# Splitting the first load of a sum of rectified rows: one row of each partition ahead of the other fifteen

## The chip, the cores and the metric

The kernel runs on one core of one Trainium2 chip. The metric is the device time of one execution in microseconds (us). Before the change it is 161.06 us, the median of three runs (161.24, 160.89 and 161.06).

## What is computed

The input `x` has the shape 32 x 512 x 1024 in float32, 67.1 MB. Every row of 1024 numbers is clamped at zero and summed:

```python
relu_x = np.maximum(x, 0)
return np.sum(relu_x, axis=-1).astype(np.float32)
```

There are 16,384 rows and as many sums, so 64 KB are written for 67.1 MB that are read.

## The kernel before

**Tiling.** The 16,384 rows are laid over 128 partitions, 128 rows to each. A block is 16 rows of every partition: 128 x 16 x 1024 float32, 8 MB, and 64 KB in one piece of memory for each partition. There are eight blocks. The first seven (`NB = 7`) are each loaded by one DMA into one of three buffers `io0` to `io2`, in turn (`NBUF = 3`). The eighth is cut into ever smaller loads: 8 rows, 4 rows, and the last four rows in four loads of 1164, 642, 120 and 122 KB, the last two into small tensors of their own (`piece0`, `piece1`).

**Two ways to sum a row.** The blocks that `TWO` lists are done in two steps: `clamp` (L117) has ScalarE (ACT in the profile) apply relu to a whole stretch of rows in place, and `total` (L125) has VectorE (DVE) reduce the stretch to one sum per row, after it has waited for the clamp. Single rows are done in one instruction, either on ACT (`act_row`, L132) or on DVE (`dve_row`, L140), with a short second instruction that reads the accumulator. `TWO = [[16], [16], [16], [8, 8], [8, 8], [7, 7], []]` gives the stretches of each block; block 0 is thus one clamp of 16 rows and one reduce of 16 rows. The seventh block and the eighth are done row by row on both engines.

**Order.** All DMAs are issued by SyncE (SP; its queue is SPq in the profile) by `load` (L99) and `store` (L110), in program order. A load into a buffer that was used before waits until DVE has counted up to the value in `freed`, which is the number of DVE instructions done when the older block of that buffer is finished. So the first three loads wait for nothing, and load 3 waits for block 0. Each load has a semaphore of its own; `act` and `dve` count the instructions of the two engines. Three stores write the sums: of block 0, of all that follows but two, and of the last two.

**The opening.** `open_without_barrier` (L238 and after) takes the first `EARLY = 1` load of SP's program out of the body and puts it ahead of SP's other instructions in the opening block. The second load and those after it stay in the body.

Of the kernel before, what the change touches and what calls it, by code (L numbers as in the profile page):

```python
# [9 lines left out]
ROWS = 16  # L10
NBUF = 3


TWO = [[16], [16], [16], [8, 8], [8, 8], [7, 7], []]
ACT = [0, 0, 0, 0, 0, 2, 9]
DVE = [0, 0, 0, 0, 0, 0, 7]

# [2 lines left out]
TAIL = [8, 4]  # L20
START_PIECE, END_PIECE = 280, 260
PIECES = [240, 244]

EARLY = 1


def kernel(tc: tile.TileContext, x: bass.AP, out: bass.AP):
    nc = tc.nc
    sems = Semaphores(tc)

    tc.close()
    tc.compile()
    nc.cur_bb = nc.bb_map[tc.start_bb_name]
    body = nc.cur_bb.bb.instructions
    ends = list(body)
    body.clear()
    n_stores = relu_sum(nc, sems, x, out)
    body.extend(ends)


    nc.cur_bb = nc.bb_map[tc.start_bb_name + "_end"]
    nc.cur_bb.bb.instructions.clear()
    nums = sorted(s.num for s in (*sems.loads, sems.act, sems.dve))
    cleared = range(nums[0], nums[-1] + 1)
    assert len(cleared) == len(nums)
    nc.sync.sem_clear(cleared)
    nc.sync.wait_ge(sems.stored, 16 * n_stores).then_inc(sems.stored, -16 * n_stores)
    open_without_barrier(tc, EARLY)


class Semaphores:
    def __init__(self, tc: tile.TileContext):
        n = len(TWO) + len(TAIL) + 2 + len(PIECES)
        self.loads = [tc.alloc_semaphore(f"load{i}") for i in range(n)]
        self.act = tc.alloc_semaphore("act")
        self.dve = tc.alloc_semaphore("dve")
        self.stored = tc.alloc_semaphore("stored")


def relu_sum(nc, sems: Semaphores, x: bass.AP, out: bass.AP):  # L60
    x_flat = x.flatten_outer_dims()
    N, D = x_flat.shape
    NT = N // P
    NB = len(TWO)
    assert N == P * NT == P * ROWS * (NB + 1)
# [3 lines left out]
    res = nc.alloc_sbuf_tensor("res", [P, NT], F32)  # L69
# [15 lines left out]
    def rows(m, n):  # L85
        if m < ROWS:
            return xf[:, m : m + n, :]
        return xv[:, m - ROWS : m - ROWS + n, :]
# [8 lines left out]
    def load(dst, src, after=None):  # L97
        nonlocal n_load
        dma = nc.sync.dma_start(out=dst, in_=src)  # L99
        if after:  # L100
            dma.wait_op(sems.dve, after[1], "sem-ge")
        dma.then_inc(sems.loads[n_load], 16)
        n_load += 1
        return sems.loads[n_load - 1]
# [10 lines left out]
    def clamp(ap, loaded):  # L115
        nonlocal n_act
        i = nc.scalar.activation(out=ap, in_=ap, func=RELU)  # L117
        if loaded is not None:
            i.wait_op(loaded, 16, "sem-ge")
        i.then_inc(sems.act, 1)  # L120
        n_act += 1

    def total(ap, m, n):
        nonlocal n_dve
        nc.vector.tensor_reduce(  # L125
            out=res[:, m : m + n], in_=ap, axis=mybir.AxisListType.X, op=ADD
        ).wait_op(sems.act, n_act, "sem-ge").then_inc(sems.dve, 1)
        n_dve += 1

    def act_row(ap, accum_out, loaded):  # L130
        nonlocal n_act
        i = nc.scalar.activation(out=ap, in_=ap, func=RELU, accum_out=accum_out)  # L132
        if loaded is not None:
            i.wait_op(loaded, 16, "sem-ge")
        i.then_inc(sems.act, 1)
        n_act += 1

    def dve_row(ap, accum_out, loaded):
        nonlocal n_dve
        i = nc.vector.tensor_scalar(  # L140
            out=ap,
            in0=ap,
            scalar1=0.0,
            scalar2=None,
            op0=MAX,
            op1=ADD,
            accum_out=accum_out,
        )
        if loaded is not None:
            i.wait_op(loaded, 16, "sem-ge")  # L150
        i.then_inc(sems.dve, 1)
        n_dve += 1

    freed = []
    m = 0
    for j in range(NB):
        buf = bufs[j % NBUF]
        loaded = load(buf[:, :, :], rows(m, ROWS), j >= NBUF and freed[j - NBUF])
        c = 0
        act_waits = dve_waits = loaded  # L160
        for n in TWO[j]:
            clamp(buf[:, c : c + n, :], act_waits)
            total(buf[:, c : c + n, :], m + c, n)
            act_waits = None
            c += n
        for _ in range(ACT[j]):
            act_row(buf[:, c, :], res[:, m + c : m + c + 1], act_waits)
            act_waits = None
            c += 1
        for _ in range(DVE[j]):  # L170
            dve_row(buf[:, c, :], res[:, m + c : m + c + 1], dve_waits)
            dve_waits = None
            c += 1
        assert c == ROWS
        freed.append((n_act, n_dve))
        m += ROWS


    buf = bufs[NB % NBUF]
    c = 0  # L180
    for n in TAIL:
        loaded = load(
            buf[:, c : c + n, :], rows(m, n), None if c else freed[NB - NBUF]
        )
# [16 lines left out]
    loaded = load(flat[:, at : at + b], src[:, :b])  # L201
# [5 lines left out]
    loaded = load(flat[:, at + end : at + 4 * D], src[:, end:])  # L207
# [30 lines left out]
def open_without_barrier(tc: tile.TileContext, n_loads: int):  # L238

    SP = mybir.EngineType.SP
    blocks = tc.nc.main_func.blocks
    opening = blocks[0].instructions
    body = next(b for b in blocks if b.name == tc.start_bb_name).instructions
    for i in list(opening):
        if isinstance(i, (mybir.InstDrain, mybir.InstEventSemaphore)):
            opening.remove(i)
    loads = [i for i in body if i.engine == SP][:n_loads]
    for i in loads:  # L250
        assert isinstance(i, mybir.InstDMACopy)
        body.remove(i)
    at = next(n for n, i in enumerate(opening) if i.engine == SP)
    opening[at:at] = loads
# [30 lines left out]
```

## Time and the profile before

| what | value |
|---|---|
| median of three runs | 161.06 us (160.89 to 161.24) |
| span of the profiled execution | 159.6 us; the page gives no other time of it |
| outside the span, by the three runs | 1.3 to 1.6 us |
| VectorE (DVE) busy | 117.6 us, 74% of the span |
| ScalarE (ACT) busy | 104.2 us, 65% |
| DMA, one queue | 67.18 MB, 98.0% of the time of 16 DMA engines |
| DMA rate over the span | 421 GB/s |

The span runs from the first instruction, the issue of the first load, to the last one. A row of the timeline gives start, duration, engine, line, operation, tiles and count, and in brackets how long the engine stood idle before it and for what. A row of the chain of waits gives the start, the duration and what the end of the program waited for at that time. "Landing" is the time from a DMA's issue to its last byte's report. In the table of windows, a DMA transfer is booked in the window in which its packets start, so that a short window can show a share far over 1.

### The profile page before, as it was taken

What the parts mean: (1) busy time and instruction counts of PE and PEld (TensorE: products, weight loads), DVE (VectorE), ACT (ScalarE), POOL (GpSimd) and SP (SyncE); (2) the same over time, 40 slices, a digit from 0 to 9 for tenths busy, and PEclk for the clock granted to TensorE, in tenths of its full rate; (3) what the DMA queues carried; (4) which work ended last, traced back from release to release, by engine and by line L of the source; (5) the groups of instructions that cost most, each with busy time, mean ns of one, the idle gap of its engine ahead of it and who ended that gap; (6) DMA issues with size and microseconds to landing.
All of it is one profiled execution on the core that took longest, in us unless ns stands there. A gap on an engine that the chain in (4) does not pass through costs nothing.

```text
span 159.6 us, 120 instructions
## 1 busy us (share of the span) xinstructions
DVE 117.6 (74%) x43; ACT 104.2 (65%) x50; POOL 0.2 (0%) x4
## 2 busy tenths in 40 slices
DVE  0000000009999499994999999999999999999986
ACT  3000059990699708996099951999329993499995
POOL 0000000000000000000000000000000000000000
DMA  7996996996997999979979969969969969798993
GB/s 279 509 526 263 526 526 263 526 509 279 526 476 312 526 394 394 526 345 443 526 328 460 526 263 526 526 263 526 509 279 526 493 296 526 337 452 382 418 412 119
DMA packets 2304, 67.18 MB, mean 421 GB/s; under 512 B 640, under 2 KB 896, under 8 KB 1024
## 3 DMA queue, kind: packets, MB, share of 16 engines
q1 hardware_dynamic: 2304, 67.18, 98.0%
HBM read 67.11 MB, written 0.07 MB: 421 GB/s over the span
## 4 chain that ended last, share of the span: by engine, by line
DMA 43%; DVE 34%; ACT 17%; another core or an unknown queue 3%; SPq 1%; issue 0%
DMA io<-in_x_dram 43%; DVE res L125 32%; ACT io L117 17%; DVE io L140 1%; SPq L99 1%; DVE piece L224 0%; DVE piece L140 0%
## 5 line engine op out<-in xcount | busy, mean ns | idle before, releaser
L125 DVE TENSOR_REDUCE res<-io 128x8 f32<-128x8192 f32 (+2 forms) x9 | 101.1, 11287 | 40.0 <-ACT io L117 40.0
L117 ACT ACTIVATE io<-io 128x8192 f32<-128x8192 f32 (+2 forms) x9 | 81.7, 9110 | 47.7 <-DMA io<-in_x_dram 47.7
L132 ACT ACTIVATE io<-io 128x1024 f32<-128x1024 f32 x20 | 20.9, 1045 | 6.0 <-DMA io<-in_x_dram 6.0
L140 DVE TENSOR_SCALAR_CACHE_REDUCE io<-io 128x1024 f32<-128x1024 f32 (+2 forms) x15 | 15.8, 1110 | 0.5 <-DMA io<-in_x_dram 0.4
L132 ACT ACTIVATION_READ_ACCUMULATOR io<-io 128x1 f32 x20 | 3.8, 188 | 0.0
L117 ACT ACT_TABLE_LOAD x1 | 1.3, 1283 | 0.1
L140 DVE DVE_READ_ACCUMULATOR io<-io 128x1 f32 x15 | 1.2, 82 | 0.0
L224 DVE TENSOR_SCALAR_CACHE_REDUCE piece<-piece 128x247 f32<-128x247 f32 x1 | 0.4, 410 | 0.0
L140 DVE TENSOR_SCALAR_CACHE_REDUCE piece<-piece 128x240 f32<-128x240 f32 x1 | 0.4, 397 | 0.0
L269 POOL MEMSET const-bfloat16-1.0<- 128x1 bf16 x1 | 0.1, 101 | 0.0
L269 POOL MEMSET const-uint8-127<- 128x1 uint8 x1 | 0.1, 101 | 0.0
L269 POOL MEMSET const-float32-0.0<- 128x1 f32 x1 | 0.1, 98 | 0.2 <-issue 0.2
L269 POOL MEMSET const-float32-1.0<- 128x1 f32 x1 | 0.1, 98 | 0.0
L224 DVE DVE_READ_ACCUMULATOR piece<-piece 128x1 f32 x1 | 0.1, 83 | 0.0
L140 DVE DVE_READ_ACCUMULATOR piece<-piece 128x1 f32 x1 | 0.1, 82 | 0.0
## 6 DMA issues: line engine op xcount, KB each, us to landing
io<-in_x_dram SPq DMA_DIRECT2D x1, 4096.0 KB, 21.6
io<-in_x_dram SPq DMA_DIRECT2D x1, 2048.0 KB, 26.1
io<-in_x_dram SPq DMA_DIRECT2D x1, 1164.0 KB, 28.4
io<-in_x_dram SPq DMA_DIRECT2D x1, 642.0 KB, 29.5
piece<-in_x_dram SPq DMA_DIRECT2D x1, 122.0 KB, 29.2
piece<-in_x_dram SPq DMA_DIRECT2D x1, 120.0 KB, 29.4
io<-in_x_dram SPq DMA_DIRECT2D x7, 26.9
out_dram<-res SPq DMA_DIRECT2D x1, 55.0 KB, 1.6
```

The costliest lines, as they stand in the source:

```text
L99: dma = nc.sync.dma_start(out=dst, in_=src)
L117: i = nc.scalar.activation(out=ap, in_=ap, func=RELU)
L125: nc.vector.tensor_reduce(out=res[:, m : m + n], in_=ap, axis=mybir.AxisListType.X, op=ADD).wait_op(sems.act, n_act, "sem-ge").then_inc(se ...
L132: i = nc.scalar.activation(out=ap, in_=ap, func=RELU, accum_out=accum_out)
L140: i = nc.vector.tensor_scalar(out=ap, in0=ap, scalar1=0.0, scalar2=None, op0=MAX, op1=ADD, accum_out=accum_out,)
L224: nc.vector.tensor_scalar(out=last[:, :], in0=last[:, :], scalar1=0.0, scalar2=None, op0=MAX, op1=ADD, accum_out=res[:, NT - 2 : NT - 1],) ...
L269: nc = _bacc.Bacc("TRN2", target_bir_lowering=False, num_devices=1)
```

## The change

The load of block 0 becomes two loads. The first takes row 0 of each partition (4 KB of each, 512 KB in all); the second takes rows 1 to 15 (60 KB of each partition, 7.5 MB). Row 0 is summed by a `dve_row`, which waits for the first of the two. Block 0's clamp and reduce shrink from 16 rows to 15 and wait for the second. There is one load semaphore more. `EARLY` stays 1, so the load that stands in the opening is now that of row 0, and the load of the 15 rows is the first one in the body.

```diff
-TWO = [[16], [16], [16], [8, 8], [8, 8], [7, 7], []]
+TWO = [[15], [16], [16], [8, 8], [8, 8], [7, 7], []]
 ...
 EARLY = 1
+
+
+FIRST = 1
 ...
-        n = len(TWO) + len(TAIL) + 2 + len(PIECES)
+        n = 1 + len(TWO) + len(TAIL) + 2 + len(PIECES)
 ...
         buf = bufs[j % NBUF]
-        loaded = load(buf[:, :, :], rows(m, ROWS), j >= NBUF and freed[j - NBUF])
         c = 0
+        if j == 0:
+            ahead = load(buf[:, :FIRST, :], rows(m, FIRST))
+            for _ in range(FIRST):
+                dve_row(buf[:, c, :], res[:, c : c + 1], ahead if c == 0 else None)
+                c += 1
+        loaded = load(
+            buf[:, c:, :], rows(m + c, ROWS - c), j >= NBUF and freed[j - NBUF]
+        )
         act_waits = dve_waits = loaded
```

## The prediction

> **What bounds the kernel now.** I read the page's DMA lines first, then the timeline for the rhythm of the loads, then the chain of waits, and last the windows at the start.
>
> ```profile
> q1 hardware_dynamic: 2304, 67.18, 98.0%
> ```
>
> One queue keeps sixteen DMA engines busy for 98% of the span. No compute engine comes near that (DVE 74%, ACT 65%). The timeline shows how regular it is; these are ACT's first instructions on newly landed data:
>
> ```profile
> 21.87 13.86 ACT L117 ACTIVATE io<-io 128x16384 f32<-128x16384 f32 x1 [20.47 <-DMA io<-in_x_dram]
> 35.76 17.22 DVE L125 TENSOR_REDUCE res<-io 128x16 f32<-128x16384 f32 x1 [35.76 <-ACT io L117]
> 41.19 13.86 ACT L117 ACTIVATE io<-io 128x16384 f32<-128x16384 f32 x1 [5.46 <-DMA io<-in_x_dram]
> 55.08 17.22 DVE L125 TENSOR_REDUCE res<-io 128x16 f32<-128x16384 f32 x1 [2.10 <-ACT io L117]
> 60.55 13.86 ACT L117 ACTIVATE io<-io 128x16384 f32<-128x16384 f32 x1 [5.50 <-DMA io<-in_x_dram]
> 74.44 66.64 DVE L125 TENSOR_REDUCE res<-io 128x16 f32<-128x16384 f32 x7 [2.14 <-ACT io L117]
> 79.90 13.95 ACT L117 ACTIVATE io<-io 128x8192 f32<-128x8192 f32 x2 [5.50 <-DMA io<-in_x_dram]
> ...
> 137.96 1.06 ACT L132 ACTIVATE io<-io 128x1024 f32<-128x1024 f32 x1 [5.04 <-DMA io<-in_x_dram]
> ...
> 147.67 1.06 ACT L132 ACTIVATE io<-io 128x1024 f32<-128x1024 f32 x1 [0.25 <-DMA io<-in_x_dram]
> ...
> 155.36 1.06 ACT L132 ACTIVATE io<-io 128x1024 f32<-128x1024 f32 x1 [0.30 <-DMA io<-in_x_dram]
> ...
> 156.95 1.06 ACT L132 ACTIVATE io<-io 128x1024 f32<-128x1024 f32 x1 [0.44 <-DMA io<-in_x_dram]
> ```
>
> The starts 41.19, 60.55 and 79.90 are 19.35 us apart: one 8 MB load lands every 19.35 us, whatever the engines do, and ACT waits 5.5 us for each. DVE's waits of 2.10 and 2.14 us are for ACT, which follows the landing. The last rows, at 137.96, 147.67, 155.36 and 156.95, show the tail's loads landing one after the other in the same stream. So the time is a start-up, 64 MB at a fixed rate, and what is left to do after the last landing.
>
> The chain of waits shows both ends of that:
>
> ```profile
> 0.00 0.38 SPq L99
> 0.38 0.05 issue
> 0.43 40.73 DMA io<-in_x_dram
> ...
> 126.91 28.43 DMA io<-in_x_dram
> 155.34 0.02 issue
> 155.37 2.02 DVE io L140 x6
> ```
>
> SP issues the first load in 0.38 us and the second at 0.43 us, though the first stands in the opening and the second in the body: the body adds no visible gap. The end is the tail's loads and 2.7 us of DVE behind them.
>
> **The change, part by part.** The profiled execution has a span of 159.6 us, and its own full time is not shown; the median run, 161.06, is 1.46 us above the span. I add each cost to the span and carry the same 1.46 us.
>
> *One DMA more in the stream.* What a DMA costs beyond its bytes can be read from the tail. Write R for the time of 8 MB at the bare rate and a for the fixed part of a DMA. Then R + a = 19.35, and the 8-row load gives R/2 + a = 147.67 - 137.96 = 9.71. So a = 2 x 9.71 - 19.35 = 0.07 and R = 19.28. Second reading: between 147.67 and 155.36, 7.69 us, the 4-row load and the 1164 KB load land, 3212 of 8192 KB: 0.392 x 19.28 = 7.56, which leaves 0.13 for two, 0.065 each. Third: the 642 KB load, 156.95 - 155.36 = 1.59, against 0.0784 x 19.28 = 1.51, leaves 0.08. So one DMA more costs 0.07 us (0.065 to 0.08). The third reading also answers for small pieces: that load takes 5 KB from each partition, the new one 4 KB, at the same distance of 64 KB. Row 0's load then takes 19.28/16 + 0.07 = 1.28 us, the other fifteen rows 18.08 + 0.07 = 18.15, together 19.43 against 19.35. **On the path: +0.07 us.** All later landings move by it, and so do ACT's starts, the reduce at 74.44 from which DVE works almost without a pause, and the end.
>
> The Trainium skill speaks against the change. Its page "DMA: Bandwidth & Descriptors" ("Rules for kernel authors") wants at least 1 MiB per DMA, and its section "Anatomy of one DMA" fits about 2.0 us of fixed cost plus bytes at 436 GB/s to each. By that the sum would be 161.06 + 2.0 = 163.1 us. The page's fit is for one DMA by itself, issued by another engine. The trace's tail, where loads are queued behind each other, charges a small DMA 0.07 us, and this is what I use.
>
> *The start.* This part is not shown: no small load opens a cold queue in this trace. What is shown is this:
>
> ```profile
> 0.00:1.00 1.00, 0.00 (x0) 0.88 (x1) 0.20 (x4) 1.00 0.00 0
> 1.00:2.00 1.00, 0.00 (x0) 0.40 (x1) 0.00 (x0) 1.00 3.01 1049
> ```
>
> No packet starts in the first microsecond after the issue (DMA share 0.00), and the first ones start in the second (3.01, booked whole at their start). The first 8 MB were landed at about 21.85; less one interval of 19.35 that is 2.5 us of start-up, waiting and report together. After the change SP issues row 0's load in the same place and the 15 rows' load at 0.43, where the second load is now. If the second's data can flow 0.43 us after the first's, it is ready 1.28 - 0.43 = 0.85 us before the first one's bytes are through: no bubble, cost 0. The bounds: at worst the second load is held up so that the DMA engines stand idle for a start of the kind seen here, 1.0 us from issue to packets. At best the start gets shorter: the packet records behind the page have the sixteen engines begin their first 64 KB packet between 1.01 and 1.81 us and take 2.50 to 3.27 us for it, where later ones take 2.42, and these first packets end between 3.96 and 4.58, a skew of 0.6 us that is kept to the end. If a small first load evened that out, up to 0.6 us could be gained. I take 0, since the nearest row, the issue at 0.43, leaves 0.85 us of cover; if that cover is gone, each tenth of a microsecond idle is a tenth at the end.
>
> *Work moved to DVE and taken from ACT.* A `dve_row` of 1024 takes 1.21 us and its accumulator read 0.08. It runs as soon as row 0 is in, about 2.5 + 1.28 = 3.8 us, where DVE stands idle until 35.76: cost 0. The clamp of 15 rows takes 15/16 of 13.86, 13.0 us, the reduce of 15 rows 15/16 of 17.22, 16.1. Block 0 is then finished at 21.94 + 13.0 + 16.1 = 51.1 instead of 53.0. Next on DVE is block 1's reduce, which waits for ACT until 55.08 either way, so this saving ends in idle time. The DVE row's wait stands at the head of DVE's queue with only the reduce of block 0 behind it, which waits far longer.
>
> *SP's queue.* One issue more, about 0.43 us, moves loads 1 and 2 from 0.43 and 0.90 to about 0.9 and 1.35; their data are wanted at about 22 and 41. Load 3, issued when block 0 is free, goes out 1.9 us earlier, but its bytes stand behind load 2's until about 60. Cost 0. The extra semaphore lengthens one range clear at the end that the last store covers. Cost 0.
>
> Sum: span 159.6 + 0.07 = 159.67, and with 1.46 around it **161.13 us**.
>
> **The rivals.**
>
> *A bubble at the start (slower).* The 15 rows' load is not ready when row 0's 1.28 us are over, and the engines idle. It decides from a delay of over 0.85 us between the two loads' first packets beyond the 0.43 of their issues. Against it: the 0.43, and that the tail's small loads follow each other at 0.07 us apiece. For it: those had been queued long before. Price up to 1.0 us: 161.13 + 1.0 = 162.1; half of it, 161.6.
>
> *A smoother start (faster).* The skew of 0.6 us shrinks since all engines have only 4 KB pieces in hand while they get going. Half of the skew gone gives 161.13 - 0.3 = 160.8, all of it 160.5. Against it: the late start of some engines need not depend on the size of their first piece.
>
> *The earlier freed buffer is worth its 1.9 us (159.2).* It would need load 3 to be late now. The unbroken 19.35 between 60.55 and 79.90, the landing of load 3, says that it is not.
>
> **How the numbers follow.** This kernel can be told from no change by about 0.2%, 0.32 us. The forecast, +0.07 with the start as it is (160.9 to 161.3): 0.60. The bubble: 0.25. The smoother start: 0.14. The freed buffer: 0.01. So faster 0.15, same 0.60, slower 0.25. The range goes from half of the smoother start's gain, 160.8, to 161.8, two thirds of the bubble's price; about 0.2 is left out, on both sides. The forecast's own range is 160.9 to 161.3.
>
> **What would show it.** In the profile after: the issue of the 15 rows' load at 0.43; ACT's first clamp at about 21.94 and of 13.0 us; the next clamps at 41.26 and 60.62; the reduce of block 0 over at 51.1 and DVE idle about 4 us behind it; 19.35 between later landings. A bubble would show as a first clamp at 22.3 or later, with everything after it equally late. A smoother start would show as a first clamp before 21.7. A change of the interval of 19.35 itself would say that I have misread what sets the rate.

## The result and the profile after

The changed kernel takes 161.38 us (median of 15 runs, 161.26 to 161.67) where the kernel before takes 161.03 (15 runs, 160.89 to 161.28). The ratio is 1.0022 with a 95% interval of 1.0015 to 1.0030: slower by 0.35 us, between 0.24 and 0.48. The profiled execution took 161.29 us, with a span of 159.9.

The timeline of the changed kernel, ACT's and DVE's first work on each block (start, duration, engine, line, operation, count, and the idle time before it):

```profile
3.85 1.22 DVE L143 TENSOR_SCALAR_CACHE_REDUCE io<-io 128x1024 f32<-128x1024 f32 x1 [3.85 <-DMA io<-in_x_dram]
...
22.18 13.00 ACT L120 ACTIVATE io<-io 128x15360 f32<-128x15360 f32 x1 [20.77 <-DMA io<-in_x_dram]
35.21 16.15 DVE L128 TENSOR_REDUCE res<-io 128x15 f32<-128x15360 f32 x1 [30.14 <-ACT io L120]
41.52 13.86 ACT L120 ACTIVATE io<-io 128x16384 f32<-128x16384 f32 x1 [6.35 <-DMA io<-in_x_dram]
55.41 17.22 DVE L128 TENSOR_REDUCE res<-io 128x16 f32<-128x16384 f32 x1 [4.05 <-ACT io L120]
60.88 13.86 ACT L120 ACTIVATE io<-io 128x16384 f32<-128x16384 f32 x1 [5.50 <-DMA io<-in_x_dram]
74.77 66.65 DVE L128 TENSOR_REDUCE res<-io 128x16 f32<-128x16384 f32 x7 [2.13 <-ACT io L120]
80.23 13.95 ACT L120 ACTIVATE io<-io 128x8192 f32<-128x8192 f32 x2 [5.49 <-DMA io<-in_x_dram]
```

The row of DVE runs at 3.85, the clamp of 15 rows takes 13.00 and the reduce 16.15, as forecast, and DVE then stands idle for 4.05 us. What is not as forecast is the place of the first clamp: 22.18 instead of 21.94; it was 21.87 before. From there on nothing more is lost: 41.52, 60.88 and 80.23 are 0.33 later than their counterparts, the same 0.33 at each, and the intervals are 19.34 to 19.36 as before. So nearly the whole loss, 0.31 of 0.33, is there when the first clamp starts at 22.18.

The chain of waits and the windows at the start (the columns of a window: its length, busy time and count of DVE, ACT and POOL, the clock, the DMA share and GB/s):

```profile
0.00 0.38 SPq L102
0.38 0.05 issue
0.43 0.42 SPq L102
0.86 0.04 issue
0.90 40.60 DMA io<-in_x_dram
```

```profile
0.00:1.00 1.00, 0.00 (x0) 0.88 (x1) 0.20 (x4) 1.00 0.00 0
1.00:2.00 1.00, 0.00 (x0) 0.40 (x1) 0.00 (x0) 1.00 0.90 168
2.00:3.00 1.00, 0.00 (x0) 0.00 (x0) 0.00 (x0) 1.00 2.01 836
3.00:4.00 1.00, 0.15 (x1) 0.00 (x0) 0.00 (x0) 1.00 1.19 504
```

The load of the 15 rows is issued at 0.43, and packets start in every window from 1 us on. The packet records confirm that there is no bubble: on the first engine to finish row 0 the last 4 KB packet is followed by the 9 ns that report it, at 2.775, and by its first 60 KB packet at 2.781; on every one of the sixteen engines the gap is under 0.1 us. The engines do not stand idle, their packets last longer. An undisturbed packet takes 159 ns for 4 KB, 1213 for 32 KB, 2267 for 60 KB and 2418 for 64 KB. Call what the packets of a load take beyond that, summed and divided by the sixteen engines, its **excess**. Before the change the first 64 KB packets have 0.59 us of excess and the other seven of that load next to none. After it, row 0's load has 0.50 and the 60 KB packets another 0.34, in the first five of the eight that each engine reads. That is 0.25 more. With 0.07 for the fixed cost it makes 0.32, and 0.33 is what the later blocks show. The sum fits so closely in this execution only: in a second profile of the same kernel (below) it makes 0.43, and the third clamp is 0.37 late. The excess is a mean over the engines, and a load has landed when the last of them has reported.

### The profile page after: what moved, and what is told of

Read it like the earlier page. It is cut to its first block, busy times and chain, and to the rows that moved or that the text cites. A ratio compares the mean times of both kernels' runs of the same rounds, so it can differ in the third digit from the quotient of the medians.

```text
span 159.9 us, 123 instructions
## 1 busy us (share of the span) xinstructions
DVE 117.8 (74%) x45; ACT 103.4 (65%) x50; POOL 0.2 (0%) x4
## 4 chain that ended last, share of the span: by engine, by line
DMA 43%; DVE 34%; ACT 17%; another core or an unknown queue 3%; SPq 1%; issue 0%
DMA io<-in_x_dram 43%; DVE res L128 32%; ACT io L120 17%; DVE io L143 1%; SPq L102 1%; DVE piece L234 0%; DVE piece L143 0%
## 5 line engine op out<-in xcount | busy, mean ns | idle before, releaser
L128 DVE TENSOR_REDUCE res<-io 128x8 f32<-128x8192 f32 (+3 forms) x9 | 100.0, 11168 | 36.3 <-ACT io L120 36.3
L120 ACT ACTIVATE io<-io 128x8192 f32<-128x8192 f32 (+3 forms) x9 | 80.9, 9015 | 48.9 <-DMA io<-in_x_dram 48.9
L143 DVE TENSOR_SCALAR_CACHE_REDUCE io<-io 128x1024 f32<-128x1024 f32 (+2 forms) x16 | 17.1, 1117 | 4.4 <-DMA io<-in_x_dram 4.3
```

The costliest lines, as they stand in the source:

```text
L128: nc.vector.tensor_reduce(out=res[:, m : m + n], in_=ap, axis=mybir.AxisListType.X, op=ADD).wait_op(sems.act, n_act, "sem-ge").then_inc(se ...
L143: i = nc.vector.tensor_scalar(out=ap, in0=ap, scalar1=0.0, scalar2=None, op0=MAX, op1=ADD, accum_out=accum_out,)
```

## The experiments

Four questions were put: is it the price of any additional DMA, the engines' work, the size of the pieces, or their place in the stream and in memory? The theories are named in the expectations. Each kernel was timed beside the kernel before. The diffs show the lines that matter; three dots stand for lines left out.

**The split in the middle of the stream.**

```diff
-TWO = [[15], [16], [16], [8, 8], [8, 8], [7, 7], []]
+TWO = [[16], [16], [15], [8, 8], [8, 8], [7, 7], []]
 ...
-        if j == 0:
+        if j == 2:
             ahead = load(buf[:, :FIRST, :], rows(m, FIRST))
```

> Block 0 whole again; block 2's load is split into row 0 and rows 1 to 15 instead. Theory A (the sixteen DMA engines start together, hinder each other until they have spread in time, and the step from 4 KB to 60 KB pieces right after the start makes them spread a second time): in the middle of a settled stream only the fixed cost of one DMA is left, 0.07 to 0.10 us over the kernel before, about 161.1, and no 60 KB packet much over 2.27 us. Theory B (60 KB pieces that begin 4 KB into each 64 KB are read more slowly by themselves): +0.35 as in the change, 161.4, with the same long 60 KB packets. Theory D (one more DMA simply costs 0.35 anywhere): 161.4, without long packets.

161.09 us against 161.06, ratio 1.0002 (0.9993 to 1.0011). The timeline:

```profile
21.84 13.86 ACT L120 ACTIVATE io<-io 128x16384 f32<-128x16384 f32 x1 [20.43 <-DMA io<-in_x_dram]
41.16 13.86 ACT L120 ACTIVATE io<-io 128x16384 f32<-128x16384 f32 x1 [5.47 <-DMA io<-in_x_dram]
60.58 13.00 ACT L120 ACTIVATE io<-io 128x15360 f32<-128x15360 f32 x1 [5.56 <-DMA io<-in_x_dram]
```

Between the second and the third row stand the two loads of block 2: 60.58 - 41.16 = 19.42, 0.07 over the 19.35 of one. That is the term of the sum, measured by itself. The excess of the 60 KB packets is 0.00. So theory D (0.35 for any DMA) and theory B (the size by itself) fall.

**8 and 8 rows.**

```diff
-TWO = [[15], [16], [16], [8, 8], [8, 8], [7, 7], []]
+TWO = [[8], [16], [16], [8, 8], [8, 8], [7, 7], []]
 ...
-FIRST = 1
+FIRST = 8
```

> Block 0 split into 8 and 8 rows (32 KB pieces both times), the first eight summed row by row on DVE in its idle time. Theory A: the engines spread during the first 32 KB piece and the second load has pieces of the same size, so only the fixed cost: +0.07, 161.1. Theory B says nothing of 32 KB pieces at an offset of 32 KB, at most +0.35. Theory D: +0.35, 161.4.

161.24, ratio 1.0014 (1.0005 to 1.0023), over what theory A said. The loads, though, are as it said: excess 0.69 in each engine's first 32 KB packet, 0.00 afterwards, and the third clamp at 60.56. The profiled execution took 161.23 us, 0.2 more than others with a third clamp at that time, and its span, 159.69 us, does not hold the difference: 1.54 us lie outside it. In the mean of its eleven runs 1.6 us lie outside the span, where every other kernel has 1.34 to 1.37, and the spans themselves are no longer than those of the kernel before (159.67 against 159.73 in the mean). So the loads behave as theory A said, and this kernel's loss arises outside the span; what it is there was not found.

**The split of the DMA alone.**

```diff
             ahead = load(buf[:, :FIRST, :], rows(m, FIRST))
-            for _ in range(FIRST):
-                dve_row(buf[:, c, :], res[:, c : c + 1], ahead if c == 0 else None)
-                c += 1
+            nc.scalar.wait_ge(ahead, 16)
+            c = FIRST
         loaded = load(...)
+        c = 0
```

> Only the DMA is split (row 0, then rows 1 to 15); ACT waits for both and clamps all 16 rows, DVE reduces all 16 as before the change, and there is no row on DVE at 3.85 us. Theories A, B and D: as the change, 161.35 to 161.4, with the same long 60 KB packets between 2.8 and 14 us. Theory C (the DVE row, or ACT's and DVE's new times, slow the loads): 161.1.

161.58, ratio 1.0033 (1.0020 to 1.0045), with an excess of 0.77 in row 0's load and 0.17 in the 60 KB packets. ACT's first clamp, now of 16 rows again:

```profile
22.40 13.86 ACT L120 ACTIVATE io<-io 128x16384 f32<-128x16384 f32 x1 [16.84 <-DMA io<-in_x_dram]
```

Theory C falls: without DVE's row the loss is there in full. It is a matter of the DMAs.

**Row 0 behind the 15 rows.**

```diff
+            loaded = load(buf[:, FIRST:, :], rows(m + FIRST, ROWS - FIRST))
+            behind = load(buf[:, :FIRST, :], rows(m, FIRST))
 ...
```

> Block 0 in two loads, but the 15 rows first and row 0 behind them. Theory A: the spread happens once, in the first 60 KB packet (about 0.59 us over the rate, as the 64 KB packet of the kernel before); the 4 KB pieces come in a settled stream: +0.07 to 0.15, 161.1 to 161.2. Theory B: the 60 KB pieces are slow again, +0.35, 161.4. Theory D: 161.4.

161.32, ratio 1.0016 (1.0007 to 1.0025), between the two. The first 60 KB packets have 0.65, near the 0.59 of the kernel before, the other 60 KB packets 0.08 and the 4 KB packets 0.11. Theory A missed this: the 4 KB pieces did not come for nothing behind a spread stream. And this kernel lost a quarter of a microsecond without a small load at the opening.

**Blocks 0 and 1 in each other's place.** Block 2, where the split cost 0.07, differs from block 0 in memory too: block 0 has 64 KB from one partition to the next, all others 448 KB. Two kernels tell place and memory apart: the split block 0 as the second block, and the split of block 1 as the first.

```diff
+        m = (ROWS, 0)[j] if j < 2 else ROWS * j
...
-    store(0, ROWS, *freed[0])
+    store(0, ROWS, *freed[1])
```

and for the first of them

```diff
-        if j == 0:
+        if j == 1:
             ahead = load(buf[:, :FIRST, :], rows(m, FIRST))
```

> The blocks 0 and 1 change places: block 1 (its partitions lie 448 KB apart in memory) is loaded first and whole, block 0 (partitions 64 KB apart) second and split into row 0 and rows 1 to 15. Theory A (a second spread is needed only because the small pieces come right at the start): the stream has settled before the split, +0.05 to 0.10, 161.1, 60 KB packets at 2.27 us. Theory B2 (60 KB pieces out of memory with 64 KB between partitions are slower by themselves; block 2, where the split cost nothing, has 448 KB): 0.2 to 0.35 us of excess in the 60 KB packets again, 161.3 to 161.4.

161.12, ratio 1.0001 (0.9993 to 1.0010); excess in the 60 KB packets 0.06.

> Blocks 0 and 1 change places, and the one that is now first, with partitions 448 KB apart, is split into row 0 and rows 1 to 15. Theory A: the split stands at the start again, so +0.25 to 0.45 as in the change, 161.3 to 161.5, with long 60 KB packets in the second load. Theory B2: 60 KB packets at the bare 2.27 us and only the fixed cost, 161.1.

161.02, ratio 1.0001 (0.9992 to 1.0010); excess 0.55 in row 0's load, 0.01 in the 60 KB packets. Its timeline beside that of the change:

```profile
21.86 13.00 ACT L120 ACTIVATE io<-io 128x15360 f32<-128x15360 f32 x1 [20.46 <-DMA io<-in_x_dram]
41.22 13.86 ACT L120 ACTIVATE io<-io 128x16384 f32<-128x16384 f32 x1 [6.36 <-DMA io<-in_x_dram]
60.58 13.86 ACT L120 ACTIVATE io<-io 128x16384 f32<-128x16384 f32 x1 [5.50 <-DMA io<-in_x_dram]
```

The same split, also at the very start, and the first clamp at 21.86 instead of 22.18. Theory A expected 161.3 to 161.5 here, theory B2 161.3 to 161.4 in the other: both are wrong by themselves. The split costs its 0.35 us neither at the start on other memory nor on this memory in second place. That the small load must come first is not shown: with row 0 behind, the time was 161.32.

**The control, and the opening alone.** Neither block is split in the control. In the other kernel row 0 of block 0 opens the stream, block 1 follows whole, and then rows 1 to 15 of block 0. The lines are of the other kernel; the control has the one that sets `m`.

```diff
+    ahead = load(bufs[1][:, :FIRST, :], rows(0, FIRST))
     freed = []
...
+        m = (ROWS, 0)[j] if j < 2 else ROWS * j
+        if j == 1:
+            c = FIRST
```

> The control for the two kernels with blocks 0 and 1 in each other's place: nothing is split, only the order is changed, so that the stream opens with 64 KB pieces 448 KB apart. Theory A2 (the split costs only where it opens the stream on memory with 64 KB between partitions): as the kernel before, 161.0 to 161.1, so that the split in this place cost nothing beyond 0.07. Theory E (the split costs 0.3 here too, but the swap gains as much): 160.7 to 160.8.

160.97, ratio 0.9994 (0.9985 to 1.0003). The swap by itself gains nothing that this can tell; 0.05 us lie between it and its split version (161.02). Theory A2 holds here.

> Row 0 of block 0 first, as in the change, but then the whole of block 1 (64 KB pieces, 448 KB apart), and only then rows 1 to 15 of block 0. Theory A2: the engines' order after the 4 KB pieces does not matter to block 1's pieces, and by the time of the 60 KB pieces the stream is settled: 161.05 to 161.15, little excess in either. Theory F (4 KB pieces 64 KB apart on a cold queue leave the engines so that whatever follows is slowed): 161.3 to 161.5, with long packets in block 1's load.

161.26, ratio 1.0008 (1.0000 to 1.0017), between the theories. Excess 0.66 in row 0's load, 0.00 in block 1's, and 0.15 in the 60 KB packets, although these come 19 us later. So it is not true that whatever follows is slowed (F), nor that the stream is settled by then (A2).

**Other memory for block 0.** Row 0's load takes the first 512 KB of `x` in one piece, the other the next 7.5 MB with 60 KB to each partition and 60 KB between them; in the second kernel the order of the two is reversed. The store of block 0 is left as it was, so that both kernels put its sums in wrong places; they serve for the times alone.

```diff
+    xa = x_flat[:P].rearrange("(p m) d -> p m d", p=P)
+    xb = x_flat[P:N1].rearrange("(p m) d -> p m d", p=P)
     def rows(m, n):
+        if m < FIRST:
+            return xa
+        if m < ROWS:
+            return xb[:, m - FIRST : m - FIRST + n, :]
```

> The change with other memory behind block 0: the first load takes the first 512 KB of x in one piece, 4 KB to each partition, the second the next 7.5 MB, 60 KB to each partition, 60 KB apart (the sums of block 0 land in other places, so they are of other rows). Theory A with the collisions caused by distances of a power of two: with 60 KB between partitions no second spread, 161.1. Theory A with collisions whatever the distance, for instance by the sheer simultaneous start: 161.3 to 161.5 as the change. Theory B2: 161.1.

160.94, ratio 0.9994 (0.9985 to 1.0003). The opening has half the excess, 0.25, but the 60 KB packets have 0.25 again, and a little more comes in the loads after them; in time it is the kernel before. Neither form of theory A foresaw both: the second spread came, and the loss did not.

> The same packed memory, but the 60 KB pieces first and the 4 KB pieces behind them (sums in other places again). If distances of a power of two cause the excess of the start (0.59 us in each engine's first 64 KB packet before, 0.65 with 60 KB pieces at 64 KB), it shrinks here to well under 0.4 and the time is at or under the kernel before, 160.8 to 161.0; if not, the excess stays at 0.55 to 0.7 and the time at 161.1 to 161.3.

161.47, ratio 1.0026 (1.0015 to 1.0036), and an excess of 0.74 in the first packets; both are above what was expected if the guess was wrong. The guess that distances of a power of two make the excess of the start is refuted: 60 KB between partitions opened no better than 64. This kernel, too, lost time without a small load at the opening.

**The change again, and a try to beat both.**

> The changed kernel once more, for a second profile of it beside the other kernels on this chip: 161.3 to 161.5. If the long 60 KB packets of the second load are what the change costs, they are there again, 0.15 to 0.4 us for each engine; if they are an accident of one execution, the time is the same without them.

161.55, ratio 1.0027 (1.0018 to 1.0036); excess 0.73 in row 0's load and 0.22 in the 60 KB packets. The long 60 KB packets are no accident of one execution, and they sit at the same place as in the first profile: most of the excess is in the third and fourth packet of each engine. The opening differs more between two executions of one kernel, 0.50 and 0.73, than between most kernels.

The same place shows in other profiles. In all six that read 60 KB pieces of block 0 with 64 KB between them, most of what these pieces lose behind the start lies in the third to fifth packet of each engine: 0.24 of 0.34 in the change, and nearly all of 0.06 and 0.15 in the two kernels that read them from 22 us on. So this part goes with the place in the load, or in the memory, rather than with the time since the stream began.

```diff
+    oa = o_flat[:P].rearrange("(p m) -> p m", p=P)
+    ob = o_flat[P:N1].rearrange("(p m) -> p m", p=P)
...
-    store(0, ROWS, *freed[1])
+    store(0, FIRST, *freed[1])
+    store(FIRST, ROWS - FIRST, *freed[1])
```

> A version meant to beat both kernels: the first load takes the first 512 KB of x in one piece (4 KB to each partition, nothing between them), then block 1 whole, then the other 7.5 MB of block 0 in 60 KB pieces; one store more puts the sums in their places. The packed first load had 0.25 us of excess per engine where the change's had 0.50 and the kernel before 0.59. Theory A2: 0.3 gained at the start, 0.07 for the load and about 0.1 for the small store given back, 160.9. If the engines are slowed by what follows, as in the kernel with the packed load and 60 KB pieces: 161.1 or more.

165.89, ratio 1.0305 (1.0282 to 1.0327). The loads are not to blame: DVE starts on the last piece at 157.74, as in the kernel before. The stores are. This is the section on DMA issues (size, and time from issue to landing), first the four stores of this kernel, then the last store of the kernel before:

```profile
out_dram<-res SPq DMA_DIRECT2D x1, 55.0 KB, 6.8
out_dram<-res SPq DMA_DIRECT2D x1, 0.5 KB, 30.7
out_dram<-res SPq DMA_DIRECT2D x1, 7.5 KB, 31.4
out_dram<-res SPq DMA_DIRECT2D x1, 1.0 KB, 7.1
...
out_dram<-res SPq DMA_DIRECT2D x1, 1.0 KB, 1.4
```

The last store, 1 KB, lands 7.1 us after its issue; in the kernel before it took 1.4. The packets themselves are not longer, and the last of them starts at 159.2 in both kernels; it is the reports that straggle in, up to 165.32 against 159.59. Ahead of this store in the queue are pieces of 4 and 60 bytes per partition, where the kernel before has 64. The two were not tried apart. And the opening did not pay either: with block 1 behind the packed row the loads end no earlier than before. No version beat the kernel before.

**All together.** The excess, and ACT's clamp of the third block, which is the same work in all kernels but one (there it has 15 rows). Excess and clamp are of one profiled execution, the ratio is of all runs:

| kernel | opening: pieces, KB between partitions, excess | 60 KB pieces behind, excess | third clamp, us | ratio |
|---|---|---|---|---|
| before | 64 KB, 64: 0.59 | none | 60.55 | 1 |
| blocks swapped, whole | 64 KB, 448: 0.50 | none | 60.51 | 0.9994 |
| split in block 2 | 64 KB, 64: 0.69 | 448: 0.00 | 60.58 | 1.0002 |
| swapped, split at the start | 4 KB, 448: 0.55 | 448: 0.01 | 60.58 | 1.0001 |
| swapped, split in the second | 64 KB, 448: 0.72 | 64: 0.06 | 60.70 | 1.0001 |
| row 0, then block 1 | 4 KB, 64: 0.66 | 64: 0.15 | 60.93 | 1.0008 |
| the change | 4 KB, 64: 0.50 | 64: 0.34 | 60.88 | 1.0022 |
| the change again | 4 KB, 64: 0.73 | 64: 0.22 | 60.92 | 1.0027 |
| DMA split alone | 4 KB, 64: 0.77 | 64: 0.17 | 61.10 | 1.0033 |
| row 0 behind | 60 KB, 64: 0.65 | 64: 0.08 | 61.02 | 1.0016 |
| 8 and 8 rows | 32 KB, 64: 0.69 | none | 60.56 | 1.0014 |
| packed row first | 4 KB, 4: 0.25 | 60: 0.25 | 60.52 | 0.9994 |
| packed, 15 rows first | 60 KB, 60: 0.74 | 60: 0.01 | 60.96 | 1.0026 |
| packed row, then block 1 | 4 KB, 4: 0.36 | 60: 0.06 | 60.57 | 1.0305 |

The profiled time less the start of the third clamp is 100.41 to 100.46 us in every profile below the first line but two: that of 8 and 8 rows, with its time outside the span, and the last, with its stores. So the fate of the others is settled before 61 us, and what is lost there is never made up.

The mean excess does not give the clamp by itself. With the DMA split alone the sixteen engines report the third block at 60.55 us in the mean, as in the change (60.56), but the last of them at 61.08 instead of 60.86. The spread between the engines is a part of the loss that the excess leaves out.

## Why the prediction was right, and where it was off

- **What bounds it.** Right: the stream of loads. Every delay at its start came out at the end undiminished, and the intervals of 19.35 us did not change.
- **One DMA more, 0.07.** Right where it was read, by a run of its own: 19.42 for the split block 2 against 19.35. But the reading was carried to block 0 on a wrong premise: the 642 KB load of the tail was said to have its pieces "at the same distance of 64 KB", and by the kernel they lie 448 KB apart, as those of all blocks but block 0 do. On memory with 448 KB the same split cost nothing that the times can tell (161.02), on block 0's it cost 0.35. The page "DMA: Bandwidth & Descriptors" of the Trainium skill ("Anatomy of one DMA"), with its 2.0 us for each DMA of another issuing engine, would have made 163.1 of the change by estimate. The runs of this case side with the row from the tail.
- **The start, 0.** This is the step that failed. The term was put at 0, with the ends +1.0 and -0.6, and measured about 0.26: 0.33 at the clamps behind the first, less 0.07. The reasoning behind the 0 looked only for idle engines, found 0.85 us of cover, and that cover held. It did not ask whether the pieces of the second load run at the full rate so early. They do not: 0.34, 0.17 and 0.22 us of excess in three executions with these loads. The rivals both missed the manner, though the slower one had the sign; the first clamp at 22.18 lies between the 21.94 of the forecast and the 22.3 that was to show a bubble.
- **Work moved between ACT and DVE, SP's queue, the earlier freed buffer: 0 each.** Right. The DMA split alone cost as much as the whole change, so the moved row has no part in it; the buffer freed 1.6 us earlier (a reduce that ends at 51.36 instead of 52.98) left the third and fourth blocks where the stream put them.
- **The number.** 161.13 was forecast for +0.07, and 161.38 came, inside the range of 160.8 to 161.8 and above the forecast's own range, which ended at 161.3. That it lies inside is luck: the range went so high for a bubble, and there was none. The direction was right, the size was 0.07 for 0.35, and 0.35 us is a little over the 0.32 that the forecast called no change. By that measure the "slower" came that had a chance of 0.25, not the "same" that had 0.60. The 1.46 us around the span mixed one run's time with another's span; time less its own span is 1.29 to 1.39 in every run of both kernels that has the two. The sum did not suffer, since it is 161.06 + 0.07 either way.

What stays open is why the packets take longer. The runs show where: 60 KB pieces of the memory with 64 KB between partitions, 0.06 to 0.34, more if a 4 KB load opened the stream, even 19 us earlier (0.15); the same pieces of the memory with 448 KB, next to none (0.00 and 0.01). The two kernels that lost time with the 60 KB pieces in front show that there is more to it. The Trainium skill's "DMA: Bandwidth & Descriptors" ("Latency and other measured facts") tells of slower copies within memory where the rows of the partitions lie a large power of two apart, from 512 KiB on, and infers, without having verified it, streams in lockstep that meet in memory. It has no row for 64 KB, and no run here shows that cause. The difference between 64 and 448 KB would go with that. The opening with 60 KB pieces 60 KB apart, 0.74, does not. The kernels that vary the distance also read other addresses, so distance and address were not told apart.

## What to carry to other kernels

Where the stream of loads is the bound, read the first landings for a lost rate as well as for a gap: busy engines can be slow ones, and in such a kernel a quarter of a microsecond lost at the start is there at the end. A load of small pieces put in front of a large one costs its fixed 0.07 us plus what the next load's pieces lose, and this second part has to be measured, since it changed from 0 to 0.3 us with the memory that was read and the place in the stream. A head start for an engine that is then idle for 30 us buys nothing.

## What the runs showed of the hardware that was not expected

The sixteen DMA engines keep to the end the lead and lag that they have when their packets run undisturbed: between the first and the last engine's report of a load lie 0.56 us at the second load of the kernel before and 0.56 at its ninth, 0.71 and 0.72 in the kernel with the DMA split alone. With block 2 split it fell from 0.56 to 0.45 within the second load, where some packets were still long, and then stayed. So the spread that the first blocks leave is still there when the last loads land.

Starting a stream cost the engines 0.25 to 0.77 us in the mean beyond the bare rate in all fourteen profiles, whatever the pieces. The lowest figures, 0.25 and 0.36, belong to the 4 KB pieces that lie next to each other in memory.
